# A row-gradient kernel at the DMA rate: in-place tiles in three buffers, with loads and stores on separate queues

## The chip, the cores and the metric

The kernel runs on one core of one Trainium2 chip. The metric is the device time of one execution in microseconds (us). The record marks an execution as slow when it takes over 1.5% more than the fastest of its kernel.

Engines have these names in the profile: DVE is VectorE, ACT is ScalarE, SP is SyncE. SPq and ACTq are the instruction streams from which SyncE and ScalarE issue DMAs; here each is also a DMA queue of its own (q1 and q10 in the profile). Sixteen DMA engines move the data of both. A *packet* in this text is one entry of the profiler's list of DMA transfers; the largest here are of 64 KB, what a load brings to one partition.

## The reference

The input is a matrix of 8192 x 8192 float32 (268.4 MB). The output has the same size: the gradient along the rows.

```python
def reference(x):
    return np.gradient(x, axis=1)
# inside a row:  out[j] = (x[j+1] - x[j-1]) / 2
# at its ends:   out[0] = x[1] - x[0],  out[m-1] = x[m-1] - x[m-2]
```

So 536.9 MB have to cross between HBM and the core's memory. There is no reuse: the work per element is one subtraction and one multiplication.

## The kernel before

One set is 256 rows, two per partition, and there are 32 sets. An input tile has 64 KB per partition, an output tile 32 KB; there are two of each (192 KB in all). All DMAs are issued on SyncE's queue.

```python
xpool = ctx.enter_context(tc.tile_pool(name="xpool", bufs=2))
opool = ctx.enter_context(tc.tile_pool(name="opool", bufs=2))
for i in range(nsets):
    x_tile = xpool.tile([P, R, m], x.dtype)                 # R = 2 rows
    nc.sync.dma_start(out=x_tile, in_=x_sets[i])            # L32: one load, 64 KB per partition
    # ... the last set is cut into 4 chunks per row ...
    for t in range(R):
        o_tile = opool.tile([P, m], out.dtype)
        nc.vector.tensor_sub(out=o_tile[:, lo:hi],          # L45
                             in0=x_tile[:, t, lo + 1 : hi + 1],
                             in1=x_tile[:, t, lo - 1 : hi - 1])
        # ... the two end columns, L51 and L57 ...
        nc.scalar.mul(out=o_tile[:, lo:hi], in_=o_tile[:, lo:hi], mul=0.5)   # L62
        nc.sync.dma_start(out=out_sets[i, :, t, c0:c1],     # L67: one store per row, 32 KB
                          in_=o_tile[:, c0:c1])
```

## Time and profile before

| | before |
|---|---|
| median of 4 runs | 1256.2 us (1253.9 to 1257.6) |
| VectorE, ScalarE busy | 45%, 36% |
| DMA queue's share of the 16 engines' time | 99.4% |
| DMA packets of 64 KB (loads), median and mean | 2418 ns, 2443 ns |
| DMA packets of 32 KB (stores), median and mean | 1213 ns, 1215 ns |

These are lines of the page of the kernel before. The DMA row gives the busy share in tenths for 40 equal slices of the span, the GB/s row what the engines moved in each slice, the last line the queue with packets, MB and its share of 16 engines' time.

```profile
span 1256.6 us, 670 instructions
...
DVE 565.4 (45%) x198; ACT 452.3 (36%) x71; POOL 0.2 (0%) x4
...
DMA  9999999999999999999999999999999999999997
GB/s 405 430 430 434 438 432 432 423 433 432 441 434 416 429 432 444 434 423 423 433 443 432 430 425 431 435 441 430 423 433 436 441 427 425 428 432 428 434 412 308
DMA packets 14693, 536.92 MB, mean 427 GB/s; under 512 B 1632, under 2 KB 1632, under 8 KB 1632
...
q1 hardware_dynamic: 14688, 536.88, 99.4%
```

The reader is to see a flat row of nines over a flat row of about 430 GB/s, with a low last slice. The compute engines are idle more than half of the time. The waits of the kernel before say for what (engine, line and what it waited for; total us, times, longest):

```profile
...
DVE o_tile L45 <- DMA out_dram<-o_tile: 656.8, 62, 21.4
DVE o_tile L45 <- DMA x_tile<-in_x_dram: 22.5, 1, 22.5
```

The first line looks like the bottleneck and is none. It says that VectorE has to wait until a store has emptied an output tile. VectorE would wait as long for anything else, since the bytes set the pace.

The windows view of the kernel before, by stretches of the span: start and end, length, busy time of DVE, ACT and POOL with instruction counts, the PE clock, the DMA share and GB/s.

```profile
...
47.00:1225.00 1178.00, 529.75 (x180) 421.67 (x61) 0.00 (x0) 1.00 1.00 431
40.00:47.00 7.00, 0.09 (x2) 7.00 (x1) 0.00 (x0) 1.00 0.82 356
47.00:62.00 15.00, 8.83 (x3) 0.74 (x2) 0.00 (x0) 1.00 1.07 463
...
1221.00:1225.00 4.00, 0.00 (x0) 0.00 (x0) 0.00 (x0) 1.00 0.84 360
1225.00:1229.00 4.00, 2.96 (x3) 0.64 (x1) 0.00 (x0) 1.00 0.44 188
1229.00:1233.00 4.00, 4.00 (x3) 3.34 (x3) 0.00 (x0) 1.00 0.64 270
1233.00:1250.00 17.00, 11.11 (x8) 11.30 (x6) 0.00 (x0) 1.00 1.01 423
1250.00:1257.00 7.00, 0.00 (x0) 0.00 (x0) 0.00 (x0) 1.00 0.23 94
```

From 47 to 1225 us the engines are full. Near the end there is a hole, in this view between 1221 and 1233 us, and after 1250 only a rest is moved.

A tally of all packets of 8 KB and more in the load and store queues (start and length of each) makes an exact account; the small packets, which it leaves out, come to under 1 us per engine. With 16 engines, *packets* is the sum of all packet times divided by 16, *idle* is the time in which fewer than 16 packets were under way (weighted by how many were missing), *overlap* is the time in which there were more. First packet + packets + idle - overlap + end = span:

| us | first packet | packets | idle, first 60 us | idle, middle | idle, last 60 us | overlap | after the last packet | span |
|---|---|---|---|---|---|---|---|---|
| before | 1.73 | 1248.16 | 0.24 | 0.32 | 6.96 | 2.57 | 1.75 | 1256.6 |

### The profile page before, as it was taken

Reading aid. Unit: us, or ns where it says so; the run is one execution under the profiler, and the core shown is the slowest. Engines: PE = TensorE matmul, PEld = TensorE weight load, DVE = VectorE, ACT = ScalarE, POOL = GpSimd, SP = SyncE. Lnnn points to the kernel's source line nnn. Section 1 sums busy time; section 2 is a strip of 40 time slices with the busy share of each in tenths; the row PEclk is TensorE's granted clock in tenths of the full one; section 3 lists DMA queues with packets and bytes.
Section 4 is the critical chain, followed back from the end, with each engine's and each line's share of the span. In section 5 each row is a group of like instructions: output and inputs, shape, how many; then the busy total and the mean of one; then the engine's idle time right before and its main releaser. Section 6 shows DMA issues by size and latency. Waiting matters only on the chain.

```text
span 1256.6 us, 670 instructions
## 1 busy us (share of the span) xinstructions
DVE 565.4 (45%) x198; ACT 452.3 (36%) x71; POOL 0.2 (0%) x4
## 2 busy tenths in 40 slices
DVE  2534553345533455334553345533455333554335
ACT  0434422344223442234422344223443234432244
POOL 0000000000000000000000000000000000000000
DMA  9999999999999999999999999999999999999997
GB/s 405 430 430 434 438 432 432 423 433 432 441 434 416 429 432 444 434 423 423 433 443 432 430 425 431 435 441 430 423 433 436 441 427 425 428 432 428 434 412 308
DMA packets 14693, 536.92 MB, mean 427 GB/s; under 512 B 1632, under 2 KB 1632, under 8 KB 1632
## 3 DMA queue, kind: packets, MB, share of 16 engines
q1 hardware_dynamic: 14688, 536.88, 99.4%
q14 instruction: 5, 0.04, 0.0%
HBM read 268.44 MB, written 268.44 MB: 427 GB/s over the span
## 4 chain that ended last, share of the span: by engine, by line
DMA 58%; DVE 23%; ACT 18%; issue 0%; DVEq 0%
DMA out_dram<-o_tile 57%; DVE o_tile L45 23%; ACT o_tile L62 18%; DMA x_tile<-in_x_dram 2%; DVEq L45 0%; DVE o_tile L57 0%; DVE o_tile L51 0%; DVEq L95 0%
## 5 line engine op out<-in xcount | busy, mean ns | idle before, releaser
L45 DVE TENSOR_TENSOR o_tile<-x_tile 128x8190 f32<-128x8190 f32 (+2 forms) x70 | 556.7, 7959 | 679.4 <-DMA out_dram<-o_tile 656.8
L62 ACT ACTIVATE o_tile<-o_tile 128x8190 f32<-128x8190 f32 (+2 forms) x70 | 451.0, 6443 | 793.6 <-DVE o_tile L45 793.6
L51 DVE TENSOR_TENSOR o_tile<-x_tile 128x1 f32<-128x1 f32 x64 | 9.8, 153 | 0.0
L57 DVE TENSOR_TENSOR o_tile<-x_tile 128x1 f32<-128x1 f32 x64 | 9.8, 153 | 0.0
L62 ACT ACT_TABLE_LOAD x1 | 1.3, 1283 | 0.7 <-PEq L84 0.7
L84 POOL MEMSET const-bfloat16-1.0<- 128x1 bf16 x1 | 0.1, 101 | 0.0
L84 POOL MEMSET const-uint8-127<- 128x1 uint8 x1 | 0.1, 101 | 0.0
L84 POOL MEMSET const-float32-0.0<- 128x1 f32 x1 | 0.1, 98 | 0.2 <-issue 0.2
L84 POOL MEMSET const-float32-1.0<- 128x1 f32 x1 | 0.1, 98 | 0.0
## 6 DMA issues: line engine op xcount, KB each, us to landing
out_dram<-o_tile SPq DMA_DIRECT2D x62, 4096.0 KB, 23.0
out_dram<-o_tile SPq DMA_DIRECT2D x8, 1024.0 KB, 8.1
x_tile<-in_x_dram SPq DMA_DIRECT2D x32, 42.5
```

Source lines behind the costliest of these rows:

```text
L45: nc.vector.tensor_sub(out=o_tile[:, lo:hi], in0=x_tile[:, t, lo + 1 : hi + 1], in1=x_tile[:, t, lo - 1 : hi - 1],)
L51: nc.vector.tensor_sub(out=o_tile[:, 0:1], in0=x_tile[:, t, 1:2], in1=x_tile[:, t, 0:1],)
L57: nc.vector.tensor_sub(out=o_tile[:, m - 1 : m], in0=x_tile[:, t, m - 1 : m], in1=x_tile[:, t, m - 2 : m - 1],)
L62: nc.scalar.mul(out=o_tile[:, lo:hi], in_=o_tile[:, lo:hi], mul=0.5,)
L84: nc = _bacc.Bacc("TRN2", target_bir_lowering=False, num_devices=1)
```

## The change

The intent: write the result over the input tile (shifted by 64 elements, so that a subtraction never overwrites what it still has to read), which frees the output tiles. Three buffers of 64 KB then fit where two and two had been. Loads keep SyncE's queue, stores move to ScalarE's, and each store is one DMA of 64 KB per partition. Instructions are issued in the order written.

```diff
-    xpool = ctx.enter_context(tc.tile_pool(name="xpool", bufs=2))
-    opool = ctx.enter_context(tc.tile_pool(name="opool", bufs=2))
+    pool = ctx.enter_context(tc.tile_pool(name="pool", bufs=3))
+    def diff(b, c0, c1):                      # SH = 64, W = 2 * m
+        # ... end columns apart ...
+        nc.vector.tensor_sub(
+            out=b[:, lo:hi],
+            in0=b[:, SH + lo + 1 : SH + hi + 1],
+            in1=b[:, SH + lo - 1 : SH + hi - 1],
+        )
+        nc.scalar.mul(out=b[:, lo:hi], in_=b[:, lo:hi], mul=0.5)
+    with tc.manual_schedule():
+        for i in range(nsets):
+            last = i == nsets - 1
+            b = pool.tile([P, SH + W], x.dtype)
+            ls = m if last else W
+            for c0 in range(0, W, ls):
+                nc.sync.dma_start(
+                    out=b[:, SH + c0 : SH + c0 + ls],
+                    in_=x_sets[i, :, c0 : c0 + ls],
+                )
+            step = m // 4 if last else m // 2
+            for c0 in range(0, W, step):
+                diff(b, c0, c0 + step)
+                if last:
+                    nc.scalar.dma_start(
+                        out=out_sets[i, :, c0 : c0 + step], in_=b[:, c0 : c0 + step]
+                    )
+            if not last:
+                nc.scalar.dma_start(out=out_sets[i], in_=b[:, 0:W])
```

More of the change, by code (lines that the diff above doesn't have):

```diff
@@ L20 @@
     R = 2
-    rows_per_set = P * R
-    nsets = n // rows_per_set
-    x_sets = x.rearrange("(s p t) m -> s p t m", p=P, t=R)
-    out_sets = out.rearrange("(s p t) m -> s p t m", p=P, t=R)
-    xpool = ctx.enter_context(tc.tile_pool(name="xpool", bufs=2))
-    opool = ctx.enter_context(tc.tile_pool(name="opool", bufs=2))
-    for i in range(nsets):
-        x_tile = xpool.tile([P, R, m], x.dtype)
-        nc.sync.dma_start(out=x_tile, in_=x_sets[i])
-        last = i == nsets - 1
-        nchunks = 4 if last else 1
-        for t in range(R):
-            o_tile = opool.tile([P, m], out.dtype)
-            csz = m // nchunks
-            for c in range(nchunks):
-                c0 = c * csz
-                c1 = c0 + csz
-                lo = max(c0, 1)
-                hi = min(c1, m - 1)
-                nc.vector.tensor_sub(
-                    out=o_tile[:, lo:hi],
-                    in0=x_tile[:, t, lo + 1 : hi + 1],
-                    in1=x_tile[:, t, lo - 1 : hi - 1],
-                )
-                if c0 == 0:
-                    nc.vector.tensor_sub(
-                        out=o_tile[:, 0:1],
-                        in0=x_tile[:, t, 1:2],
-                        in1=x_tile[:, t, 0:1],
-                    )
-                if c1 == m:
-                    nc.vector.tensor_sub(
-                        out=o_tile[:, m - 1 : m],
-                        in0=x_tile[:, t, m - 1 : m],
-                        in1=x_tile[:, t, m - 2 : m - 1],
-                    )
-                nc.scalar.mul(
-                    out=o_tile[:, lo:hi],
-                    in_=o_tile[:, lo:hi],
-                    mul=0.5,
-                )
-                nc.sync.dma_start(
-                    out=out_sets[i, :, t, c0:c1], in_=o_tile[:, c0:c1]
-                )
@@ new lines @@
+    SH = 64
+    W = R * m
+    nsets = n // (P * R)
+    x_sets = x.rearrange("(s p t) m -> s p (t m)", p=P, t=R)
+    out_sets = out.rearrange("(s p t) m -> s p (t m)", p=P, t=R)
+    pool = ctx.enter_context(tc.tile_pool(name="pool", bufs=3))
+    def diff(b, c0, c1):
+        lo, hi = c0, c1
+        if c0 % m == 0:
+            lo = c0 + 1
+            nc.vector.tensor_sub(
+                out=b[:, c0:lo],
+                in0=b[:, SH + c0 + 1 : SH + c0 + 2],
+                in1=b[:, SH + c0 : SH + c0 + 1],
+            )
+        if c1 % m == 0:
+            hi = c1 - 1
+        nc.vector.tensor_sub(
+            out=b[:, lo:hi],
+            in0=b[:, SH + lo + 1 : SH + hi + 1],
+            in1=b[:, SH + lo - 1 : SH + hi - 1],
+        )
+        if hi < c1:
+            nc.vector.tensor_sub(
+                out=b[:, hi:c1],
+                in0=b[:, SH + hi : SH + c1],
+                in1=b[:, SH + hi - 1 : SH + c1 - 1],
+            )
+        nc.scalar.mul(out=b[:, lo:hi], in_=b[:, lo:hi], mul=0.5)
```

## The prediction

> **What bounds the kernel now.** It only moves bytes. The page shows VectorE busy 45% and ScalarE 36%; the queue list gives the one hardware queue 99.4% of the 16 DMA engines' time; the windows view gives 431 GB/s and a DMA share of 1.00 from 47 to 1225 us. The chain of waits names stores (57%), subtractions (23%) and multiplications (18%), but it runs through buffers that wait for a store to land: DMA bandwidth seen from VectorE. 656.8 us of VectorE's idle time is of this kind and costs nothing.
>
> The packets of the trace: a 64 KB load packet takes 2418 ns at the median (2443 mean), a 32 KB store packet 1213, an 8 KB one 309. Together they make 1249.3 us on each of 16 engines, of a 1256.6 us span. 64 KB in 2418 ns is 433.7 GB/s for 16 engines. The Trainium skill, "DMA: Bandwidth & Descriptors", section "Where 436 GB/s comes from", gives 435.2 GB/s as the ports' ceiling; the trace agrees, within 1% of it in the steady part. So the steady part, 94% of the time, has next to nothing to win.
>
> **What the change does.**
> - Store packets grow from 32 KB to 64 KB: two of 1213 ns become one, estimated at 2418 as for loads. 3968 of them, 8 ns each, over 16 engines: 2 us.
> - Loads and stores get their own queues. The same page, "Issuing engines are not separate DMA queues", says they still share the same 16 engines and interleave. I expect no bandwidth from it, and little loss from mixing directions.
> - Start: today both loads are in by about 42 us and the DMA share is 0.82 from 40 to 47. A third load fills this: 1.3 us. The first store leaves later (44 us for 38.3) without harm.
> - End: the share is 0.72 from 1225 to 1257, 9 us lost, 4 to 5 of them the last landing and shutdown. The hole of about 4 us at 1221 to 1233 is the last output tiles waiting for buffers. In the new kernel the previous set's store is still queued while the last set is computed, so the hole closes: 4 us.
> - Compute: a 4095-element subtraction costs an estimated 4.42 us, a multiplication 3.62 (lines through the 8190 and 2047 ones), so 21 us from landing to store per set, against 38.9 us of DMA per set. Three buffers in rotation keep a transfer in flight. Off the path.
>
> **Sum.** 1255.2 - 2 - 1.3 - 4 gives 1248; with something for mixing, I predict 1249 us, 8 in 10 between 1240 and 1261. Faster by over 2% (under 1230): 4%. Within 2%: 92%. Slower by over 2%: 4%.
>
> **What would show it.** DMA share 1.00 and 429 to 434 GB/s through the middle; no slice under 420 but the first and last; about 10,370 packets, 1,152 of them small; packet times summing to 1246 us per engine, if packets on two queues are still timed one by one; VectorE near 585 us busy; no hole before the last stores, the last slice over 330 GB/s.
>
> **What would make it wrong.** Two queues switching at every 64 KB packet could cost a gap each time (50 ns per packet would be 2%), or HBM could turn around between reads and writes more often: the middle would fall under 425 GB/s. Or reads and writes of two queues could overlap in an engine[...]: the middle would exceed 440. Or load and store rotation could fall into step and leave both queues empty at once: dips in the slices every 39 us.

## The result

The changed kernel takes 1251.07 us (median of 4 runs, 1248.6 to 1251.7); the kernel before 1256.2 us. The ratio is 0.9957, with a 95% interval from 0.9937 to 0.9978: the same within 2%, and a gain of 0.4% that is clear of the noise. Ratios in this text are the mean time of one kernel's fast runs over that of the other's fast runs of the same rounds, so they are not quite the ratio of the medians.

The same lines of the page of the changed kernel:

```profile
span 1246.8 us, 665 instructions
...
DVE 584.6 (47%) x260; ACT 464.9 (37%) x133; POOL 0.2 (0%) x4
...
DMA  9999999999999999999999999999999999999998
GB/s 404 437 435 437 427 421 433 437 437 435 438 435 437 437 435 416 429 437 437 437 433 437 437 435 437 435 414 433 437 437 435 435 438 435 437 435 433 426 426 343
DMA packets 10373, 536.92 MB, mean 431 GB/s; under 512 B 1152, under 2 KB 1152, under 8 KB 1152
...
q1 hardware_dynamic: 4752, 268.44, 49.9%
q10 hardware_dynamic: 5616, 268.44, 49.7%
```

The work is now split evenly over two queues, the same bytes come in 10,373 packets for 14,693, and many slices stand at 437 where few did. The windows of the changed kernel, the middle and the end:

```profile
...
47.00:1220.00 1173.00, 551.84 (x244) 441.08 (x124) 0.00 (x0) 1.00 1.00 433
...
1223.00:1229.00 6.00, 4.95 (x4) 2.11 (x2) 0.00 (x0) 1.00 1.00 425
1229.00:1240.00 11.00, 4.54 (x3) 5.53 (x3) 0.00 (x0) 1.00 1.01 427
1240.00:1243.00 3.00, 0.00 (x0) 0.00 (x0) 0.00 (x0) 1.00 0.26 109
1243.00:1247.00 4.00, 0.00 (x0) 0.00 (x0) 0.00 (x0) 1.00 0.04 16
```

There is no hole before the last stores in this execution. The last 7 us move almost nothing: the tally shows that from 1242.6 us on a single DMA engine is working, and it ends at 1245.6 us, 5 us after most of the others. The kernel before ends in the same way (one engine alone for about 1.5 us).

The account of the two executions:

| us | first packet | packets | idle, first 60 us | idle, middle | idle, last 60 us | overlap | after the last packet | span |
|---|---|---|---|---|---|---|---|---|
| before | 1.73 | 1248.16 | 0.24 | 0.32 | 6.96 | 2.57 | 1.75 | 1256.6 |
| changed | 1.74 | 1240.80 | 0.20 | 0.21 | 4.57 | 1.89 | 1.15 | 1246.8 |

Packets give 7.4 us of the 9.8 between these two executions, the end most of the rest. But 9.8 overstates the gain; the medians differ by 5.1. The profiled execution of the changed kernel is the fastest of its four, 2.5 us under their median. That of the kernel before is a long one: in 29 executions of it the device time is 1.7 to 1.8 us more than the span, so the span of 1256.6 belongs to about 1258.4 us, 2.2 over the median. The kernel before was profiled once, so how much of its 1248.16 us of packets a median execution has is not known.

Of the 7.4 us, 2.0 are the larger store packets: 3968 pairs of 1213 ns became 3968 of 2418 ns, 8 ns less each, over 16 engines. The other 5.4 are packets that took longer than the median of their size. I call this *stretch*: in the kernel before it sums to 7.7 us per engine, 6.4 of it on loads, in the changed kernel to 2.3.

The stretch has a place. Of the 6.4 us on loads in the kernel before, 5.4 fall on the last 16 of a load's 128 packets, and 0.6 on the very first packets of the run. In that kernel all loads and stores are in one queue, and all engines go from a block of loads to a block of stores once per set. An engine that arrives at this turn a little later than the others finishes its last load packet in up to 3.7 us instead of 2.42. These are packets of one such turn, in the raw list of the trace (start us, bytes, ns); the last two started 0.8 and 1.1 us after the first store packets, which came at 390.2 us:

```
387.612  65536  2418
388.853  65536  2438
388.917  65536  3260
390.998  65536  3474
391.287  65536  3414
```

In the changed kernel the same thing happens once, after 44 us of loads alone: the first store is issued at 44.5 us, the 16 load packets that start at about 46 us take about 1 us longer each (1.0 us per engine), and the first store packets follow at 49.2 us. After that loads and stores take turns packet by packet, and few packets are stretched (0.6 us per engine in all, 1.3 in the second profile, e0).

### The profile page after: what moved, and what is told of

The parts are those of the page before. It is cut to its first block, busy times and chain, and to the rows that moved or that the text cites. A ratio compares the mean times of both kernels' runs of the same rounds, so it can differ in the third digit from the quotient of the medians.

```text
span 1246.8 us, 665 instructions
## 1 busy us (share of the span) xinstructions
DVE 584.6 (47%) x260; ACT 464.9 (37%) x133; POOL 0.2 (0%) x4
## 2 busy tenths in 40 slices
DMA packets 10373, 536.92 MB, mean 431 GB/s; under 512 B 1152, under 2 KB 1152, under 8 KB 1152
## 4 chain that ended last, share of the span: by engine, by line
DMA 75%; DVE 16%; another core or an unknown queue 4%; ACT 3%; issue 0%; SPq 0%; DVEq 0%
DMA b<-in_x_dram 38%; DMA out_dram<-b 37%; DVE b L46 16%; ACT b L57 3%; DVE b L39 0%; DVE b L52 0%; SPq L66 0%; DVEq L39 0%
## 5 line engine op out<-in xcount | busy, mean ns | idle before, releaser
L57 ACT ACTIVATE b<-b 128x4095 f32<-128x4095 f32 (+1 forms) x132 | 463.6, 3512 | 747.8 <-DVE b L46 747.8
L46 DVE TENSOR_TENSOR b<-b 128x4095 f32<-128x4095 f32 (+1 forms) x132 | 567.0, 4295 | 4.5
L39 DVE TENSOR_TENSOR b<-b 128x1 f32<-128x1 f32 x64 | 9.9, 155 | 642.3 <-DMA b<-in_x_dram 642.3
L52 DVE TENSOR_TENSOR b<-b 128x1 f32<-128x1 f32 x64 | 10.2, 159 | 2.2
## 6 DMA issues: line engine op xcount, KB each, us to landing
b<-in_x_dram SPq DMA_DIRECT2D x31, 47.7
out_dram<-b ACTq DMA_DIRECT2D x31, 46.6
```

The lines of the kernel that those rows point to most:

```text
L39: nc.vector.tensor_sub(out=b[:, c0:lo], in0=b[:, SH + c0 + 1 : SH + c0 + 2], in1=b[:, SH + c0 : SH + c0 + 1],)
L46: nc.vector.tensor_sub(out=b[:, lo:hi], in0=b[:, SH + lo + 1 : SH + hi + 1], in1=b[:, SH + lo - 1 : SH + hi - 1],)
L52: nc.vector.tensor_sub(out=b[:, hi:c1], in0=b[:, SH + hi : SH + c1], in1=b[:, SH + hi - 1 : SH + c1 - 1],)
L57: nc.scalar.mul(out=b[:, lo:hi], in_=b[:, lo:hi], mul=0.5)
```

## Experiments

Each experiment was timed against the kernel before in the same rounds: e0 to e3 on one chip, e4 to e8 on a second, e9 on a third. The table gives the results, packets, stretch and idle time from one profiled execution each (those of the kernel before always from its one profile); *stretch* is the packet time above the medians, per engine.

| run | what | median us | ratio to before (95%) | packets | stretch | idle: middle, last 60 us |
|---|---|---|---|---|---|---|
| before | | 1256.2 | 1 | 1248.2 | 7.7 | 0.3, 7.0 |
| changed | | 1251.1 | 0.9957 (0.9937 to 0.9978) | 1240.8 | 2.3 | 0.2, 4.6 |
| e0 | changed, again | 1251.4 | 0.9959 (0.9943 to 0.9975) | 1241.8 | 3.3 | 0.2, 6.9 |
| e1 | before, stores on ScalarE's queue | 1340.0 | 1.0669 (1.0649 to 1.0689) | 1286.2 | 45.8 | 40.7, 7.9 |
| e2 | changed, one queue | 1249.6 | 0.9947 (0.9932 to 0.9963) | 1242.6 | 4.1 | 0.2, 3.4 |
| e3 | changed, stores of one row | 1248.3 | 0.9937 (0.9922 to 0.9952) | 1243.8 | 3.3 | 0.3, 1.8 |
| e4 | changed, two buffers | 1355.7 | 1.0787 (1.0761 to 1.0813) | 1285.6 | 47.1 | 62.1, 0.2 |
| e5 | changed, no compute (result wrong) | 1256.0 | 0.9987 (0.9960 to 1.0015) | 1243.8 | 5.2 | 0.2, 8.7 |
| e7 | changed, late stores of one row | 1248.3 | 0.9939 (0.9917 to 0.9962) | 1241.4 | 2.7 | 0.2, 3.9 |
| e8 | one queue and stores of one row | 1256.6 | 0.9999 (0.9979 to 1.0020) | 1245.3 | 4.8 | 0.3, 6.0 |
| e9 | e1 with equal packets | 1342.6 | 1.0692 (1.0673 to 1.0712) | 1288.0 | 45.5 | 46.0, 7.8 |

### e0: the changed kernel again

No edit.

> The changed kernel once more, to have it on the same chip as the next three and to see how far its profile repeats. Ratio to the kernel before 0.993 to 0.998. If the gain comes from the packets: load packets 2427 ns in the mean again (2443 before), all packets 1241 us per engine (1248.2 before). If it comes only from the ends, the packets of this run would sum to 1246 us or more and the idle time at the end would be where it differs.

Measured: 1251.35 us, ratio 0.9959. The packets sum to 1241.8 us, 6.3 less than before, so the lower sum of packets repeats. The idle time of the last 60 us does not: it is 6.9 us here. The windows of this execution at its end show why:

```profile
...
1223.00:1229.00 6.00, 0.00 (x0) 0.00 (x0) 0.00 (x0) 1.00 0.99 419
1229.00:1235.00 6.00, 4.79 (x4) 1.96 (x2) 0.00 (x0) 1.00 0.45 191
1235.00:1240.00 5.00, 4.70 (x3) 4.17 (x3) 0.00 (x0) 1.00 0.96 395
1240.00:1245.00 5.00, 0.00 (x0) 1.51 (x1) 0.00 (x0) 1.00 1.01 419
1245.00:1250.00 5.00, 0.00 (x0) 0.00 (x0) 0.00 (x0) 1.00 0.11 46
```

Here the hole that the changed kernel's first profile had lost is back, 0.45 from 1229 to 1235 us. The last half of the last load landed at 1230 us, just as the last queued stores ended, and nothing could move until its first chunk was computed: 3.6 us of idle engines, for 3.9 in the kernel before. So the end gave 2.4 us in one of these two executions and nothing in the other. What repeats is the packets.

### e1: the kernel before with its stores on ScalarE's queue

```diff
-                nc.sync.dma_start(
+                nc.scalar.dma_start(
                     out=out_sets[i, :, t, c0:c1], in_=o_tile[:, c0:c1]
                 )
```

> Kernel before, only the store queue moved to ScalarE's; stores stay 32 KB per partition, tiles stay apart, two buffers each. Theory TURN (on one queue all engines turn from loads to stores at each set, and the loads of the engines that come late are stretched; two queues mix packet by packet and have no such turn): load packets fall from 2443 to about 2427 ns in the mean, slow ones (over 30 ns above the median) from 254 to under 100, packets sum to 1243 us per engine (1248.2 less 4 of loads and 1 of stores), ratio about 0.996 to 0.997. Rival SIZE (the gain is the 64 KB store packets, and the buffers): nothing changes, ratio 1.000, slow load packets stay near 250.

Both theories miss, and by far: 6.7% slower. Two lines of this kernel's page (span, and GB/s by slice):

```profile
span 1335.5 us, 667 instructions
...
GB/s 408 432 353 408 397 404 408 410 414 399 394 398 418 408 408 408 404 412 408 393 408 397 404 408 424 393 417 368 408 413 400 396 394 410 422 406 410 398 340 377
```

The rate is low all along and not at one place. The DMA issues (KB each, median us from issue to landing; some lines have the landing time alone), first of the kernel before, then of this one:

```profile
...
out_dram<-o_tile SPq DMA_DIRECT2D x62, 4096.0 KB, 23.0
...
x_tile<-in_x_dram SPq DMA_DIRECT2D x32, 42.5
```

```profile
...
out_dram<-o_tile ACTq DMA_DIRECT2D x62, 4096.0 KB, 25.4
...
x_tile<-in_x_dram SPq DMA_DIRECT2D x32, 28.7
```

On one queue a load stands in line behind the two stores issued before it and lands after 42.5 us. On its own queue it lands after 28.7 us, and the stores are later for it (25.4 for 23.0). The load is not needed earlier, since two input tiles are filled ahead, and once it is in, no transfer is left behind which the next wait could hide. The timeline of this kernel around one such moment (start us, length, instruction; in brackets the wait before it and for what; SPq's line merges four loads issued from 632.76 us on):

```profile
...
608.19 0.34 ACTq L67 DMA_DIRECT2D out_dram<-o_tile  x1
623.91 8.69 DVE L45 TENSOR_TENSOR o_tile<-x_tile 128x8190 f32<-128x8190 f32 x1 [22.68 <-DMA out_dram<-o_tile]
...
632.76 124.03 SPq L32 DMA_DIRECT2D x_tile<-in_x_dram  x4
633.59 8.69 DVE L45 TENSOR_TENSOR o_tile<-x_tile 128x8190 f32<-128x8190 f32 x1 [0.85 <-DMA out_dram<-o_tile]
639.69 0.34 ACTq L67 DMA_DIRECT2D out_dram<-o_tile  x1
```

At 623.91 a store has landed and the subtraction of the next row starts. Only one store, that issued at 608.19, is still under way; alone it is moved at the full rate of 4 MB in under 10 us. The next load is issued at 632.76, when the subtraction has read the last of the input tile. The store has just ended then. The windows of the same stretch (columns as before):

```profile
...
618.00:632.00 14.00, 8.09 (x1) 0.00 (x0) 0.00 (x0) 1.00 1.04 449
632.00:634.50 2.50, 1.65 (x4) 1.87 (x1) 0.00 (x0) 1.00 1.25 419
634.50:640.00 5.50, 5.50 (x1) 5.16 (x1) 0.00 (x0) 1.00 0.88 381
640.00:643.50 3.50, 2.42 (x3) 1.19 (x1) 0.00 (x0) 1.00 0.91 300
643.50:660.00 16.50, 0.00 (x0) 5.84 (x1) 0.00 (x0) 1.00 0.95 413
591.00:632.20 41.20, 17.62 (x7) 14.06 (x2) 0.00 (x0) 1.00 0.98 407
```

The tally has about half of the engines empty from 632 to 634 us (8.5 of 16), load packets of 3.2 us for 2.42 after it (the restart), and again 3.2 us for those that start at about 642 us, the last before the packets of the next store, which was issued at 639.69 into an empty queue. That is also the window with 300 GB/s. Idle 1.3 us (40.7 over 31 sets) and stretch 1.4 us (44.4 on loads over 31 sets) per set come to 2.7 us, about the 2.5 us by which the period of 41.2 us exceeds the 38.75 us that a set's packets (8 of 2418 ns and 16 of 1213 on each engine) need. This is the last case that the prediction had named for being wrong (both queues empty at once, dips every 39 us), only in a kernel with the old tiles.

### e2: the changed kernel on one queue

```diff
+    def load(i):
+        ...                                   # the load as before, on nc.sync
     with tc.manual_schedule():
+        tiles = [load(0), load(1), load(2)]
         for i in range(nsets):
             ...
-            if not last:
-                nc.scalar.dma_start(out=out_sets[i], in_=b[:, 0:W])
+            if not last:
+                nc.sync.dma_start(out=out_sets[i], in_=b[:, 0:W])
+            if 1 <= i and i + 2 < nsets:
+                tiles.append(load(i + 2))
```

> Changed kernel with everything on one queue, stores issued one set ahead of the load that waits for them so that the queue never runs dry; store packets stay 64 KB. TURN: the slow load packets come back (about 250, mean near 2443 ns, 4 to 5 us per engine), packets sum to 1245 to 1246 us, ratio 0.998 to 1.000. SIZE: load packets of before had another cause, slow ones stay under 100 and the ratio stays at the changed kernel's 0.996.

Measured: 0.9947, at least as fast as the changed kernel, and packets of 1242.6 us. The theory that one queue brings back the whole stretch falls: it is 4.1 us, against 2.3 and 3.3 in the two profiles of the changed kernel and 7.7 in the kernel before (203 slow packets, not 250). So the second queue is not what the time is won by. With three buffers one queue, in the right order, does as well.

### e3: the changed kernel with stores of one row

```diff
-                nc.scalar.dma_start(out=out_sets[i], in_=b[:, 0:W])
+                for c0 in range(0, W, m):
+                    nc.scalar.dma_start(
+                        out=out_sets[i, :, c0 : c0 + m], in_=b[:, c0 : c0 + m])
```

> Changed kernel with each store cut into two of one row (32 KB per partition), both issued where the one was. Packets alone: 7936 of 1213 ns for 3968 of 2418 ns is 2.0 us more per engine, so a ratio 0.0016 above the changed kernel's in the same rounds, 0.997 to 0.998. SIZE in its strong form (store size gives all the gain): ratio 1.000. TURN: slow load packets stay under 100.

The packets behave as expected (1243.8, which is 2.0 more than in e0), and the time does the opposite: 0.9937, the lowest ratio of all, in a narrow range (1248.0 to 1248.9; e0 took 1249.2 to 1252.6 in the same rounds). The sign that TURN had named failed too: 148 load packets were slow, not under 100 (100 in e0). The idle time at the end is 1.8 us. The reason stands in the landing times of the changed kernel and of this one:

```profile
...
b<-in_x_dram SPq DMA_DIRECT2D x31, 47.7
out_dram<-b ACTq DMA_DIRECT2D x31, 46.6
```

```profile
...
out_dram<-b ACTq DMA_DIRECT2D x62, 4096.0 KB, 48.4
...
b<-in_x_dram SPq DMA_DIRECT2D x31, 33.1
```

With equal packets a load and a store that are under way together take 47.7 and 46.6 us. With stores in packets of half the size the load takes 33.1. The tally shows the share: from 632 to 656 us, with both queues at work, loads hold 11.2 of the 16 engines here, against 7.9 from 630 to 656 us in the changed kernel. Turns go by the packet, so the queue with the larger packets gets more. The last load then lands 35 us before the end (23 in the changed kernel's first profile, 20 in e0), stores are still queued while the last set is computed, and the hole is gone.

### e4: the changed kernel with two buffers

```diff
-    pool = ctx.enter_context(tc.tile_pool(name="pool", bufs=3))
+    pool = ctx.enter_context(tc.tile_pool(name="pool", bufs=2))
```

> Changed kernel with two buffers for three. In the run of the kernel before with only the store queue moved, both queues ran empty once per set: 40.7 us of idle engines in the middle and about 44 us of stretched load packets. Theory DRY (two queues share the engines packet by packet, so a set's load and store end together and with few buffers nothing is left to move; the third buffer prevents it): idle time in the middle over 10 us, load packets over 2480 ns in the mean, ratio 1.02 to 1.07. Rival SPLIT (that loss came from something else in the old tiles, such as the two output tiles; two buffers leave 25 us of one buffer's compute hidden under the other's 52 us of transfer): idle in the middle under 2 us, ratio 0.995 to 1.005.

Measured: 1.0787, 62.1 us idle in the middle, load packets of 2552 ns in the mean. The theory DRY holds, and its own upper bound of 1.07 was too low. SyncE's queue of this kernel waits for one thing:

```profile
...
SPq L66 <- DMA out_dram<-b: 1249.8, 30, 45.6
```

A load can be issued only when the store of its own buffer has landed, and at that time the other buffer is being computed. Both queues are empty for 2.0 us per set (62.1 over 31): from the end of the store to the first packet of the load that waited for it. The estimate under SPLIT, that 52 us of transfer leave room enough, had added lengths and not asked where in time they lie.

### e5: the changed kernel without compute

```diff
             for c0 in range(0, W, step):
-                diff(b, c0, c0 + step)
                 ...  # and the stores read b at SH + c0
```

> Changed kernel without its subtractions and multiplications: every tile is stored as it was loaded, so the result is wrong on purpose. If compute is off the path, as predicted: within 3 us of the changed kernel, ratio 0.993 to 0.997, packets 1241 to 1243 us per engine. If compute holds the stores back anywhere but in the last set: over 6 us faster, ratio under 0.991.

Without any arithmetic the kernel is not faster. Its ratio of 0.9987 is outside the range I gave and above the changed kernel's 0.9959, though that comes from other rounds and the intervals touch; its runs go from 1249.9 to 1259.6 us. So compute does not set the pace; that was the question. Whether it costs something in the last set, where in e0 the stores wait for it, this run cannot tell, since its transfers mix differently. Between its profile and that of e0 lie 3.6 us: 1.9 are packet stretch and 1.7 idle time in the last 60 us. Why it is so was not pursued.

### e7: late stores of one row

```diff
             if not last:
-                nc.scalar.dma_start(out=out_sets[i], in_=b[:, 0:W])
+                piece = m if i >= nsets - 4 else W
+                for c0 in range(0, W, piece):
+                    nc.scalar.dma_start(
+                        out=out_sets[i, :, c0 : c0 + piece], in_=b[:, c0 : c0 + piece])
```

> Changed kernel with only the stores of sets 28 to 30 cut into two of one row, so that the last load, which takes turns with them packet by packet, gets two thirds of the engines for a half, lands earlier and leaves stores queued for the time in which the last set is computed. Theory END (the row stores everywhere won 2 to 3 us over the changed kernel by closing the hole before the last stores, and paid 2.0 us in packets for it): idle in the last 60 us under 4 us, packets 1241 to 1242 us, ratio 0.992 to 0.993, the fastest so far. Rival LUCK (the hole comes and goes, and the row stores' gain was something else): ratio as the changed kernel's, 0.995 to 0.996.

Packets (1241.4) and idle time at the end (3.9, nearly all of it in the last 6 us, no hole) are as expected, and the ratio of 0.9939 is a little above the range and not below e3's. Its interval (0.9917 to 0.9962) also holds the 0.995 to 0.996 of LUCK, so the time alone does not decide between the two. The hole is closed as meant in this profile; that the 2 us of packets saved against e3 show in the time is not shown. This run and e3 have the lowest ratios of the correct kernels here, 0.6% under the kernel before.

### e8: one queue and stores of one row

The edit is that of e2 with the store cut as in e3.

> The one-queue form of the changed kernel with its stores cut into two of one row: 32 KB store packets behind 64 KB loads on one queue, as in the kernel before, but with three in-place buffers. The kernel before had 254 slow load packets and 7.5 us per engine of stretch; the one-queue form with 64 KB stores had 203 of both kinds and 4.1. If small stores behind the loads are the cause: stretch back near 7 us, packets 1247 to 1249 us, ratio 0.998 to 1.000. If the old order of tiles and buffers is: stretch stays near 4 us, packets 1244.5 to 1245.5, ratio 0.9955 to 0.997.

Measured: 0.9999, the time of the kernel before. The packets (1245.3) are within the range for the theory that the tiles matter, the ratio within that for small stores, so neither is settled by it. (The 7.5 us in the expectation leave out the 8 KB packets.) What it shows: one queue alone loses nothing (e2), small stores alone lose nothing (e3), both together lose the whole gain. From e2, which differs by the size of the stores alone, the profile is 5.2 us longer: 2.0 are packet size, 0.7 stretch (4.8 for 4.1) and 2.6 idle time at the end (6.0 for 3.4). The profiled execution is the fastest of its six, so these terms show the direction and not the whole of the loss. As in the kernel before, 3.7 of its 4.7 us of load stretch fall on the last 16 packets of a load.

### e9: two queues with equal packets, old tiles

```diff
-        x_tile = xpool.tile([P, R, m], x.dtype)
-        nc.sync.dma_start(out=x_tile, in_=x_sets[i])
+        x_tile = xpool.tile([P, R, m + 16], x.dtype)
+        nc.sync.dma_start(out=x_tile[:, :, 0:m], in_=x_sets[i])
```

(On top of e1. A padded row ends the contiguous run, so a load goes in packets of 32 KB.)

> The kernel before with its stores on ScalarE's queue (ratio 1.067), and its input tile padded by 64 bytes per row, so that a load of two rows goes in packets of 32 KB, as the stores do, and not of 64 KB. Theory SHARE (the two queues take turns packet by packet, so 64 KB loads got two thirds of the engines, the stores landed late, the output tiles came back late, and both queues ran empty once per set): with equal packets the stores land sooner, issue to landing of a load rises from 28.7 us to over 33, idle engines in the middle fall from 40.7 us to under 20, ratio under 1.04. Rival QUEUE (two queues with these tiles are slow whatever their packets): idle in the middle stays over 35 us, ratio 1.06 to 1.07.

The share did shift, and the time did not. The landing times of this run:

```profile
...
x_tile<-in_x_dram SPq DMA_DIRECT2D x32, 8192.0 KB, 34.7
out_dram<-o_tile ACTq DMA_DIRECT2D x62, 4096.0 KB, 26.0
```

The load now takes 34.7 us, as expected (loads hold 8.0 of 16 engines from 646 to 663 us, where both queues are at work; 10.4 from 645 to 660 us in e1), but the idle time in the middle is 46.0 us and the ratio 1.0692, both as the rival QUEUE had them. So it is not the share that makes e1 slow. The load is still in long before 42.5 us, when the kernel before gets it, and the next one still cannot be issued until a store has landed and a subtraction of 8.7 us has run. One queue would then be good for the old tiles because it keeps the load back behind the stores, as work for the time in which nothing new can be issued. This last step is read from the timelines and landing times; no run has tested it by itself.

## Why the prediction was right, point by point

- **The bound: right.** The engines were full and stayed full: DMA share 1.00 and 433 GB/s in the middle (429 to 434 had been predicted), VectorE 584.6 us busy (585), 10,373 packets (10,370). The Trainium skill, "DMA: Bandwidth & Descriptors", section "Where 436 GB/s comes from", puts the ports' ceiling at 435.2 GB/s. The trace agrees: no stretch of many sets goes over it, and single slices at 437 or more are packets booked where they start. At 2418 ns per 64 KB packet the whole matrix takes 1238 us each way together (8192 packets over 16 engines), so all that a change with packets of this size could win was under 1.5%.
- **Store packets, 2 us: right.** 1213 x 2 against 2418 ns, 3968 times, over 16 engines. e3, with the same stretch as e0, gives it back to the tenth.
- **"I expect no bandwidth from it, and little loss from mixing directions": wrong in sign, and the largest term that was not in the sum.** Stretch fell by 5.4 us (4.4 in e0), from the one profile of the kernel before. No single part of the change carries this. With the new tiles and order, but one queue and small stores, it is 4.8 us (e8, for 7.7); with large stores 4.1 (e2); with two queues 2.3 and 3.3. So the largest step, 2.9 us, came with the tiles, the buffers and the order in which loads are issued, and no run separates these. The steps are of single profiles, and two of the same kernel differ by 1.0. What happens in the engines or in HBM when they turn from loads to stores, no run shows.
- **Start, 1.3 us: wrong.** The 0.82 from 40 to 47 us was a packet booked elsewhere. The tally has 0.24 us of idle time in the first 60 us before and 0.20 after. There was nothing to win.
- **End, 4 us: half right.** The hole was there (3.9 us), and closed in one profile of the changed kernel (idle 4.6 for 7.0, the rest being the engines that end late) and not in the other (6.9). The step that fails is "the previous set's store is still queued while the last set is computed": loads and stores share the engines evenly and end together, so this holds by luck. In the profiles of e3 and e7 it holds, by the shares that row stores give.
- **Compute off the path, and no dry queues: right** (e5; 0.2 us idle in the middle). The parts were right too: a subtraction takes 4.42 us and a multiplication 3.62, and the first store is issued at 44.5 us (44). It needs the third buffer: with two, the kernel is 7.9% slower than the kernel before (e4).

The sum came to 6.2 us and the medians differ by 5.1. That is in part luck: two terms of 5.3 us together were too large and one of about 5 us was missing. Two expected signs failed with it: two slices, 416 and 414, lie under 420, and all packets together, counted as the prediction counted them, sum to 1241.7 us per engine and not to 1246.

## What to carry to other kernels

When the DMA engines are full, first work out what the packets alone take: here 1238 of 1256 us, so no rearrangement of such packets could give 2%. Queues and packet sizes still matter as *order*. In these runs one queue was a line in which a transfer could be held back as later work; two queues took turns by the packet, and ran dry unless a further buffer was waiting (the same move of the stores to a second queue cost 6.7% with the old buffers and nothing with three). Judge idle DMA time by the packets themselves, not by windows a few packets long.

## What the Trainium skill lacked or had wrong

All five points belong to the page "DMA: Bandwidth & Descriptors".

- Section "Issuing engines are not separate DMA queues" says that issuing from several engines only saves the sequencer's issue time. The runs agree that the engines and their total rate are the same, but the order changes: moving the stores to a second queue made the kernel before 1.0669 times as slow (e1), with 40.7 us of idle engines.
- Section "Queues, rings and completion order" says that an engine takes turns between queues by the packet. The trace agrees, taking its packets of 32 and 64 KB for the page's; the page lacks the consequence that packet size is a share: with 32 KB store packets for 64 KB ones beside 64 KB loads, loads held 11.2 of 16 engines for 7.9, and a load landed after 33.1 us for 47.7 (e3).
- The page has nothing on the stretch of loads at a turn from loads to stores: up to 3.7 us for a packet of 2.42, 7.7 us per engine in all packets of the kernel before, 44 us on the loads of e1.
- Section "Why small descriptors are slow (HBM only)" treats the cost per packet as a matter of small ones. It is measurable at full size: about 8 ns, from 2418 ns for 64 KB and 1213 for 32 KB.
- Section "Latency and other measured facts" says that DMA engines 7 and 15 are usually slower, and as a best guess lays it to the path of DMAs issued from GpSimd. Here no DMA is issued from GpSimd, and the changed kernel's two profiles and that of the kernel before still end with one engine alone, for 1.5 to 3.4 us. The trace doesn't name engines, so whether it is one of these two is open.
